# A third PSUM bank from another pool, and a new layout and order for the second FFN product of a decoder layer

## The chip, the cores and the metric

The kernel runs on one NeuronCore of a Trainium2 chip. Its engines run side by side, each with an instruction queue of its own that it works through in order: TensorE (PE in the profile, its weight loads PEld) multiplies matrices into PSUM, VectorE (DVE) and ScalarE (ACT) work element by element on PSUM and SBUF, GpSimd (POOL) on SBUF alone, and SyncE (SP) issues DMA transfers, which ScalarE and GpSimd can issue too. The metric is the device time of one execution in microseconds, as the median of several runs.

## The reference

The reference computes one decoder layer on a sequence of 1024 positions and 1024 channels in float32: RMS norm, an input projection, two kinds of attention with gates, an output projection with a residual, and then the feed-forward part, which is what this document is about:

```python
h2 = rms_norm(x, norm_ffn_g[layer])
gu = h2 @ w_ffn_in[layer]                       # (1024, 1024) @ (1024, 5632)
x = x + (jax.nn.silu(gu[..., :D_FF]) * gu[..., D_FF:]) @ w_ffn_down[layer]
return rms_norm(x, norm_final_g)                # D_FF = 2816
```

So the first FFN product makes a gate g and a value u for each of 2816 hidden channels, the hidden activation is a = silu(g) * u, and the second FFN product takes a, (1024, 2816), back to 1024 channels.

## The kernel before

**Precision.** Each float32 operand is split into a high part, which ScalarE rounds to the format that TensorE takes (L99), and a low part, the rest, which VectorE subtracts (L100). A product is three matmuls: high x high, high x low, low x high. A matmul here takes 128 x 128 weights and 512 columns and fills one PSUM bank. There are eight banks: six in the pool `psd` (tag d, the function `pd()`), two in `psf` (tag f). The pair `psf` is used for transposes and, earlier in the kernel, for the projections of the gates.

**First FFN product.** The hidden channels are worked in 22 blocks of 128 (j = 0 to 21). Blocks 0 and 1 are computed plainly. Each block from 2 on, the function `up`, uses a scheme with seven half-size products instead of eight, on the split activations (`hT_t`), and on sums of them (`tT`: T2, T3, T4) and of the weights (S12, S34, made by GpSimd and split). The seven products, each 12 matmuls (L299), accumulate in three banks b1, b2, b3; between them VectorE and ScalarE read the banks:

- b1: A1 x B11, copied to c1 (L1122); then A1 x B21 is added, and from b1 come a sigmoid (L1130) and a multiplication by it (tile sg, L1037), the last reader of b1;
- b2: S12 x T2, then v2 = b2 + c1; S34 x T3, then v3 = b2 + c1; A22 x T4, then a1 = b2 + c1;
- b3: S12 x T1, then a2 = b3 + v3; S34 x B22, then b3 + v2, the second half's gate.

The results go to DRAM: for blocks 2 to 17 in pairs to `left_dram`, as seven kinds of operands that are sums of quarters (`left_rows`, tile f1, L1162), for blocks 0, 1 and 18 to 21 to `a_dram`. The planner that lays out the instructions overlaps neighbouring blocks: on TensorE the first product of block j+2 comes between the products of block j and those of block j+1.

**Second FFN product.** First the plain rows of block 0: eight row tiles by two halves, 16 banks of three matmuls (L103 to L105), each copied out of its bank into the accumulator `acc` by ScalarE (first half, L1222) or VectorE (second half, L1224). Then seven products (function `product`, L1257), each over eight pairs of blocks: for each pair the left half and the right half of a raw operand are loaded by SyncE (L1246, L1252), split, and multiplied into four banks, 12 matmuls. After each product `into` adds its four banks to one or two quarters of `acc` on VectorE (L1227). During the second of them the residual is added (L1236). Last come the plain rows of blocks 1 and 18 to 21, with the final norm.

**Memory and order.** Pools are stacks, on the left or on the right of SBUF. A pool opened where others have been closed lies over their tiles, and `reuse_waits="tile"` makes each of its tiles wait for those old tiles that it overlaps, and for no other. Before the pool `down` there lay, from the left: `hT_t` (64 KB of each partition), `tT` (48 KB), and the pool `up` (s, s34, a22, c1, v2, v3, sg1, two buffers of a, and the S12 operands, 52 KB together); on the right f1 (8 KB) and two raw weights of odd blocks (8 KB). In the kernel before, `down` starts with `acc` as one tile of 32 KB, over `hT_t`; raw operands (seven buffers of 4 KB) and split ones (11 of 2 x 4 KB) follow as they come. The order on each engine is made by a planner, from the order in the program, what depends on what, and its own estimate of times. `tc.issue_after(ins)` tells it that an instruction may not come before `ins` on its engine's queue.

Of the kernel before, what the change touches and what calls it, by code (L numbers as in the profile page):

```python
# [8 lines left out]
F32 = mybir.dt.float32  # L9
F32R = mybir.dt.float32r  # L10
I32 = mybir.dt.int32
AF = mybir.ActivationFunctionType
ALU = mybir.AluOpType
PSUM = bass.MemoryType.PSUM

P = 128
D = 1024
S = 1024
KT = D // P
NT = S // P  # L20
HALF = 512
# [26 lines left out]
def layer_kernel(  # L48
# [16 lines left out]
    nc = tc.nc  # L65
# [3 lines left out]
    def pool_of(name, bufs, side="left"):  # L69
        return tc.tile_pool(name=name, bufs=bufs, side=side, reuse_waits="tile")  # L70
# [20 lines left out]
    def nm(s):  # L91
        uid[0] += 1
        return f"{s}_{uid[0]}"

    def pd():
        return psd.tile([P, HALF], F32, tag="d", name=nm("pd"))
# [169 lines left out]
    def reserve(pool, *places):  # L266
        for tag, shape, dtype, bufs in places:
            for _ in range(bufs):
                pool.tile([P] + shape, dtype, tag=tag, name=nm(tag), bufs=bufs)
# [836 lines left out]
    with pool_of("up", 1) as fpool:  # L1106
        reserve(fpool, ("s", [KT, P], F32, 2), *[("s34" + n, [KT, P], F32R, 1) for n in "hl"],
                *[("a22" + n, [4, P], F32R, 1) for n in "hl"],
                *[(n, [HALF], F32, 1) for n in ("c1", "v2", "v3", "sg1")], ("a", [S], F32, 2))

        def tmp(n):
            return fpool.tile([P, HALF], F32, tag=n, name=nm(n), bufs=1)

        def up(j, todo, half):
            A1, S12, S34, A22 = left_side(fpool, *(odd if j == PLAIN + 1 else raws(j)), 2, 1)
            b1, b2, b3 = pd(), pd(), pd()
            a = fpool.tile([P, S], F32, tag="a", name=nm("a"), bufs=2)
            a1, a2 = a[:, :HALF], a[:, HALF:]
            c1, v2, v3, sg1 = [tmp(n) for n in ("c1", "v2", "v3", "sg1")]
            prod(b1, A1[:, :4], B11, True)  # L1120
            with tc.issue_after(s12_hi[0].ins) if j == PLAIN else ExitStack():
                nc.scalar.activation(out=c1[:], in_=b1[:], func=AF.Copy)  # L1122
            prod(b2, S12[:, 4:], T2, True)
            vi = from_bank(v2[:], b2, c1)
            if todo:
                with tc.issue_after(vi.ins):
                    left_rows(*todo, 1)
            prod(b1, A1[:, 4:], B21)

            nc.scalar.activation(out=sg1[:], in_=b1[:], func=AF.Sigmoid)  # L1130
            gi = from_bank(sg1[:], b1, sg1, ALU.mult)
            if todo:
                with tc.issue_after(gi.ins):
                    left_rows(*todo, 2)
            prod(b2, S34[:, :4], T3)
            from_bank(v3[:], b2, c1)
            prod(b3, S12[:, :4], T1, True)
            ai = from_bank(a2, b3, v3)
            if half:
                with tc.issue_after(ai.ins):  # L1140
                    left_rows(None, half, None, 0)
            prod(b2, A22, T4)
            from_bank(a1, b2, c1)
            nc.gpsimd.tensor_tensor(out=a1, in0=a1, in1=sg1[:], op=ALU.mult)
            prod(b3, S34[:, 4:], B22)
            gt2, sg2 = tmp("v3"), tmp("sg1")
            from_bank(gt2[:], b3, v2)
            nc.scalar.activation(out=sg2[:], in_=gt2[:], func=AF.Sigmoid)
            nc.gpsimd.tensor_tensor(out=sg2[:], in0=gt2[:], in1=sg2[:], op=ALU.mult)
            nc.gpsimd.tensor_tensor(out=a2, in0=a2, in1=sg2[:], op=ALU.mult)  # L1150
            return a[:].rearrange("p (b c) -> p b c", b=2)

        def left_rows(n, p, q, part):

            if part == 0:
                ops = [(2, p[:, 0], p[:, 1], ALU.subtract)]
            elif part == 1:
                ops = [(0, p[:, 1], q[:, 1], ALU.add)]
            else:
                ops = [(1, f1[:, 0], p[:, 0], ALU.subtract), (3, q[:, 0], f1[:, 1], ALU.subtract)]  # L1160
            for i, x_, y_, op in ops:
                nc.vector.tensor_tensor(out=f1[:, i], in0=x_, in1=y_, op=op)  # L1162
            if part == 2:
                nc.gpsimd.dma_start(out=rows_of(left_dram[n, 3:7]), in_=f1[:])

        todo, one = None, None
        for j in range(PLAIN, NFF):
            n, second = divmod(j - 2, 2)
            a = up(j, todo, one if second and n < len(TWO_ROWS) else None)
            todo = None  # L1170
            if n >= len(TWO_ROWS):
                nc.gpsimd.dma_start(out=a_dram[j], in_=a.rearrange("p b c -> p (b c)"))
            elif second:
                nc.gpsimd.dma_start(out=rows_of(left_dram[n, 1:3]), in_=a)
                todo = (n, one, a)
            else:
                nc.gpsimd.dma_start(out=left_dram[n, 0], in_=a[:, 0])
                one = a
# [3 lines left out]
    h_ctx.__exit__(None, None, None)  # L1182


    with pool_of("down", 1) as fpool:
        acc = fpool.tile([P, NT, D], F32, name="acc", bufs=1)

        def operand(raw):

            w = Pair(*[fpool.tile([P, 2, HALF], F32R, tag="o" + n, name=nm("o" + n), bufs=11) for n in "hl"])  # L1190
            split(w.hi[:], w.lo[:], raw)
            return w

        def raw_rows():
            return fpool.tile([P, 2, HALF], F32, tag="or", name=nm("raw"), bufs=7)

        def whole(j):

# [11 lines left out]
        def plain_rows(js, evac):  # L1210
            both = [whole(j) for j in js]
            for t in range(NT):
                for ch in range(2):
                    pt = pd()
                    for n, (a, w) in enumerate(both):
                        mm3(pt[:], a[:, t * P:(t + 1) * P], w[:, ch * HALF:(ch + 1) * HALF],
                            n == 0, n == len(both) - 1)
                    evac(t, ch, acc[:, t, ch * HALF:(ch + 1) * HALF], pt)

        def first_rows(t, ch, out, pt):  # L1220
            if ch == 0:
                nc.scalar.activation(out=out, in_=pt[:], func=AF.Copy)  # L1222
            else:
                nc.vector.tensor_copy(out, pt[:])  # L1224

        def add(out, bank, op=ALU.add):
            nc.vector.tensor_tensor(out=out, in0=out, in1=bank[:], op=op)  # L1227

        plain_rows([0], first_rows)

# [2 lines left out]
        def residual(t):  # L1233
            xr = fpool.tile([P, D], F32, tag="xf", name=nm("xr"), bufs=3)
            last_xr[0] = nc.gpsimd.dma_start(out=xr[:], in_=x1_dram[t])
            nc.vector.tensor_tensor(out=acc[:, t], in0=acc[:, t], in1=xr[:], op=ALU.add)  # L1236

        def product(left, right, banks, each=None):


            new = banks is None
            banks = banks or [pd() for _ in range(NT // 2)]
            last = len(TWO_ROWS) - 1
            for n, two in enumerate(TWO_ROWS):
                raw = raw_rows()
                nc.sync.dma_start(out=raw[:, 0], in_=left_dram[n, left])  # L1246
                if isinstance(right, tuple):
                    j, b = two[right[0]], right[1]
                    src = w_ffn_down[j * P:(j + 1) * P, b * HALF:(b + 1) * HALF]
                else:  # L1250
                    src = right_dram[n, right]
                nc.sync.dma_start(out=raw[:, 1], in_=src)  # L1252
                w = operand(raw[:])
                for t, bank in enumerate(banks):
                    l, r = w[:, 0, t * P:(t + 1) * P], w[:, 1]
                    for i, (p, q) in enumerate(((l.hi, r.hi), (l.hi, r.lo), (l.lo, r.hi))):
                        nc.tensor.matmul(bank[:], p, q, start=new and n == 0 and i == 0, stop=n == last and i == 2,  # L1257
                                         skip_group_check=True)
                if each:
                    each(n)  # L1260
            return banks

        def into(banks, *blocks, op=ALU.add):
            for t, bank in enumerate(banks):
                for th, ch in blocks:
                    add(acc[:, th * NT // 2 + t, ch * HALF:(ch + 1) * HALF], bank, op)

        A11, A12, A22, S1, S2, S3, S4 = range(7)
        T1, T3, T4, T2 = range(4)
# [17 lines left out]
        def last_rows(t, ch, out, pt):  # L1287
# [7 lines left out]
                return  # L1295
            ss = small.tile([P, 1], F32, tag="ss", name=nm("ss"))
            nc.vector.tensor_tensor(out=ss[:], in0=parts[0][:], in1=parts[1][:], op=ALU.add)
            nc.vector.tensor_tensor(out=xf[:], in0=acc[:, t, :], in1=gainf[:], op=ALU.mult)
            r = rstd(ss, True)
            for c in range(2):  # L1300
                cs = slice(c * HALF, (c + 1) * HALF)
# [40 lines left out]
```

## Time and profile before

| | |
|---|---|
| median of 3 runs | 1468.48 us (1467.93 to 1469.89) |
| profiled execution, its own time | 1468.82 us |
| span in its profile | 1467.1 us |
| TensorE busy | 1441.3 us, 98% of the span |
| VectorE, ScalarE, GpSimd busy | 956.6, 553.3, 504.1 us |
| blocks of the first product with seven products | about 854 to 1241 us |
| seven products of the second | about 1250 to 1404 us |

A row of the profile names a line of the kernel (L299), an engine, an operation and tiles, written `out<-in`. In the rows in order of time the first number is the start in us from the beginning of the span, the second the duration, and what stands in brackets is how long the engine had been idle before it and what ended that. In the chain of waits a row is a start, a duration and an instruction, followed by `x` and a count where several in a row are merged. Tiles of one tag show one name, so v2 and v3 are both `v`.

### The profile page before, as it was taken

To read this page: it belongs to the slowest core of one execution; us is meant where nothing else is said; L and a number is where in the kernel's file an instruction comes from. 1 tells how busy PE (TensorE), PEld (TensorE's weight loads), DVE (VectorE), ACT (ScalarE), POOL (GpSimd) and SP (SyncE) were. 2 spreads that over 40 slices of the span, in tenths; PEclk is the share of its full clock that TensorE was granted. 3 is DMA by queue.
4 is the path that set the end of the run, shared out by engine and by line. 5 is a ranking of instruction groups with operands and counts; after the bars stand their busy time and mean duration, and the time that the engine had idled before them with its cause. 6 is when DMAs were issued, how large, how long until landed. Compare 5 with 4: busy or idle time off the path is not lost. (4 is left out here: it accounts for less than half of the span.)

```text
span 1467.1 us, 18389 instructions
## 1 busy us (share of the span) xinstructions
PE 1441.3 (98%) x6876; PEld 1162.5 (79%) x6876; DVE 956.6 (65%) x1336; ACT 553.3 (38%) x824; POOL 504.1 (34%) x438
## 2 busy tenths in 40 slices
PE   8999999999999999999999999999999999999997
PEld 7898888877677776788887778888888887788886
DVE  6484654359889999846528865555556555876555
ACT  5333332236656423354315432223223323543333
POOL 1020444535533321110146166666666665000000
PEclk9999999999999999999999999999999999999999
DMA  7232454575543461265759312323233332986502
GB/s 231 72 101 79 144 166 124 139 212 130 129 122 102 168 206 36 80 233 170 293 201 367 106 58 80 107 93 104 98 108 108 107 103 88 384 287 210 164 29 86
DMA packets 165785, 213.58 MB, mean 146 GB/s; under 512 B 13760, under 2 KB 115136, under 8 KB 165440
## 3 DMA queue, kind: packets, MB, share of 16 engines
q1 hardware_dynamic: 129376, 119.06, 26.2%
q0 software_dynamic: 15344, 55.59, 10.4%
q10 hardware_dynamic: 20976, 37.76, 8.2%
q8 instruction: 54, 0.88, 0.3%
q14 instruction: 35, 0.29, 0.1%
HBM read 146.32 MB, written 66.06 MB: 145 GB/s over the span
## 5 line engine op out<-in xcount | busy, mean ns | idle before, releaser
L299 PE MATMUL pd<-hT_t,wh 128*128 128x512 f32 x856 | 265.0, 390 | 1.4 <-DVE sg L1037 0.6
L299 PE MATMUL pd<-tT,wh 128*128 128x512 f32 x768 | 235.1, 389 | 0.7 <-ACT wh L99 0.6
L100 DVE TENSOR_TENSOR wl<-wr,wh 128x1024 fp32r<-128x1024 f32 (+2 forms) x110 | 131.2, 1194 | 127.9 <-ACT wh L99 127.3
L99 ACT ACTIVATE wh<-wr 128x1024 fp32r<-128x1024 f32 (+2 forms) x110 | 95.4, 867 | 285.6 <-PE pd L299 166.2
L299 PEld LDWEIGHTS pd<-hT_t,wh 128*128 128x128 f32 x856 | 160.0, 188 | 37.8 <-DVE sg L1037 4.7
L299 PEld LDWEIGHTS pd<-tT,wh 128*128 128x128 f32 x768 | 144.0, 188 | 31.4 <-ACT wh L99 1.0
L299 PE MATMUL pd<-hT_t,wl 128*128 128x512 f32 x428 | 166.5, 389 | 0.0
L299 PE MATMUL pd<-tT,wl 128*128 128x512 f32 x384 | 147.6, 389 | 0.0
L105 PE MATMUL pf<-hT_t,wl 128*128 128x512 f32 x288 | 114.5, 398 | 0.0
L103 PE MATMUL pf<-hT_t,wh 128*128 128x512 f32 x288 | 114.1, 396 | 0.0
L104 PE MATMUL pf<-hT_t,wh 128*128 128x512 f32 x288 | 113.7, 395 | 0.0
L100 DVE TENSOR_TENSOR ol<-raw,oh 128x1024 fp32r<-128x1024 f32 x66 | 79.6, 1223 | 45.8 <-ACT oh L99 38.5
L99 ACT ACTIVATE wh<-s 128x1024 fp32r<-128x1024 f32 x58 | 61.4, 1060 | 118.3 <-POOL s L286 91.3
L285 POOL TENSOR_TENSOR s<-wr 128x512 f32<-128x512 f32 x29 | 60.4, 2084 | 123.9 <-DMA wr<-in_w_in_dram 71.0
L99 ACT ACTIVATE oh<-raw 128x1024 fp32r<-128x1024 f32 x66 | 69.2, 1060 | 87.4 <-PE pd L1257 66.8
L299 PEld LDWEIGHTS pd<-hT_t,wl 128*128 128x128 f32 x428 | 80.3, 188 | 16.9
L100 DVE TENSOR_TENSOR wl<-s,wh 128x1024 fp32r<-128x1024 f32 x58 | 72.2, 1246 | 32.3 <-ACT wh L99 32.3
L1257 PE MATMUL pd<-ol,oh 128*128 128x512 f32 x224 | 87.2, 390 | 1.7 <-DVE ol L100 1.7
L1257 PE MATMUL pd<-oh,ol 128*128 128x512 f32 x224 | 86.3, 389 | 0.0
L984 POOL TENSOR_TENSOR r<-r 128x512 f32<-128x512 f32 x32 | 44.2, 1391 | 120.7 <-DMA r<-in_w_ffn_down_dram 119.3
L299 PEld LDWEIGHTS pd<-tT,wl 128*128 128x128 f32 x384 | 72.1, 188 | 15.0
L1257 PE MATMUL pd<-oh 128*128 128x512 f32 x224 | 83.9, 389 | 0.0
(277 smaller groups left out, 3068.4 us busy)
## 6 DMA issues: line engine op xcount, KB each, us to landing
wr<-in_w_in_dram SPq DMA_DIRECT2D x46, 512.0 KB, 4.7
wr<-in_w_ffn_in_dram SPq DMA_DIRECT2D x44, 512.0 KB, 3.8
raw<-left_dram SPq DMA_DIRECT2D x56, 256.0 KB, 5.3
g_dram<-fst ACTq DMA_DIRECT2D x32, 256.0 KB, 2.5
land<-g_dram SPq DMA_DIRECT2D x16, 512.0 KB, 3.4
r<-in_w_ffn_down_dram SPq DMA_DIRECT2D x8, 1024.0 KB, 10.4
right_dram<-r POOLq DMA_DIRECT2D x8, 1024.0 KB, 6.2
left_dram<-f POOLq DMA_DIRECT2D x8, 1024.0 KB, 4.7
```

The costliest lines, as they stand in the source:

```text
L99: last_hi[0] = nc.scalar.activation(out=hi, in_=src, func=AF.Copy)
L100: return nc.vector.tensor_tensor(out=lo, in0=src, in1=hi.bitcast(F32), op=ALU.subtract)
L103: nc.tensor.matmul(psum, w.hi, m.hi, start=start, stop=False)
L104: nc.tensor.matmul(psum, w.hi, m.lo, start=False, stop=False)
L105: last_mm[0] = nc.tensor.matmul(psum, w.lo, m.hi, start=False, stop=stop)
L285: nc.gpsimd.tensor_tensor(out=s12[:, :4], in0=u1, in1=u2, op=ALU.add)
L299: last_mm[0] = nc.tensor.matmul(bank[:], p, q, start=first and k == 0 and n == 0, stop=k == 3 and n == 2, skip_group_check=True)
L984: nc.gpsimd.tensor_tensor(out=out, in0=p, in1=q, op=ALU.subtract)
L1257: nc.tensor.matmul(bank[:], p, q, start=new and n == 0 and i == 0, stop=n == last and i == 2, skip_group_check=True)
```

## The change

The third bank b3 of each block with seven products is taken from `psf`. In the second FFN product the accumulator becomes eight tiles of one row tile each: rows 0 and 1 lie in a new pool `early` on the right, beside two raw buffers; in the left pool the places are reserved in a fixed sequence: rows 2 to 5, twelve split operands high and twelve low, two raw buffers, the tiles for the residual and the gain, rows 6 and 7, and five raw buffers, of which one is skipped on the first turn. Raw buffers are nine instead of seven, split operands twelve instead of eleven. And the splits get a told order: in the first product the split of operand n (0 to 7) comes, on each of the two engines, after that engine's copy of the plain rows' row tile 2n + 1 (at most the last, 7); in the later products the low halves from the fourth operand on come after the last add of the product before.

```diff
         def up(j, todo, half):
-            b1, b2, b3 = pd(), pd(), pd()
+            b1, b2, b3 = pd(), pd(), psf.tile([P, HALF], F32, tag="f", name=nm("pf"))
...
-    with pool_of("down", 1) as fpool:
-        acc = fpool.tile([P, NT, D], F32, name="acc", bufs=1)
+    with pool_of("down", 1) as fpool, pool_of("early", 1, side="right") as epool:
+        def rows(pool, *ts):
+            for t in ts:
+                acc[t] = pool.tile([P, D], F32, tag=f"acc{t}", name=nm("acc"), bufs=1)
+
+        acc = [None] * NT
+        rows(epool, 0, 1)
+        rows(fpool, 2, 3, 4, 5)
+        reserve(fpool, *[("o" + n, [2, HALF], F32R, 12) for n in "hl"], ("os", [2, HALF], F32, 2),
+                ("xf", [D], F32, 3), ("gain", [D], F32, 1))
+        rows(fpool, 6, 7)
+        reserve(fpool, ("or", [2, HALF], F32, 5))
+        fpool.tile([P, 2, HALF], F32, tag="or", name=nm("raw"), bufs=5)
...
-            w = Pair(*[fpool.tile([P, 2, HALF], F32R, tag="o" + n, name=nm("o" + n), bufs=11) for n in "hl"])
+            w = Pair(*[fpool.tile([P, 2, HALF], F32R, tag="o" + n, name=nm("o" + n), bufs=12) for n in "hl"])
...
+        turn = [0]
+
         def raw_rows():
-            return fpool.tile([P, 2, HALF], F32, tag="or", name=nm("raw"), bufs=7)
+            places = [(epool, "oe", 2)] * 2 + [(fpool, "os", 2)] * 2 + [(fpool, "or", 5)] * 5
+            pool, tag, bufs = places[turn[0] % 9]
+            turn[0] += 1
+            return pool.tile([P, 2, HALF], F32, tag=tag, name=nm("raw"), bufs=bufs)
...
+        emptied = [[], []]
+
         def first_rows(t, ch, out, pt):
             if ch == 0:
-                nc.scalar.activation(out=out, in_=pt[:], func=AF.Copy)
+                emptied[0].append(nc.scalar.activation(out=out, in_=pt[:], func=AF.Copy))
             else:
-                nc.vector.tensor_copy(out, pt[:])
+                emptied[1].append(nc.vector.tensor_copy(out, pt[:]))
...
         def product(left, right, banks, each=None):
...
-                w = operand(raw[:])
+                after = [q[min(2 * n + 1, NT - 1)].ins for q in emptied]
+                if n >= 3 and last_add[0]:
+                    after[1] = last_add[0].ins
+                with tc.issue_after(after[0]), tc.issue_after(after[1]):
+                    w = operand(raw[:])
...
         def into(banks, *blocks, op=ALU.add):
             for t, bank in enumerate(banks):
                 for th, ch in blocks:
-                    add(acc[:, th * NT // 2 + t, ch * HALF:(ch + 1) * HALF], bank, op)
+                    last_add[0] = add(acc[th * NT // 2 + t][:, ch * HALF:(ch + 1) * HALF], bank, op)
```

The other lines of the diff only write `acc[t][...]` for `acc[:, t, ...]`.

More of the change, by code (lines that the diff above doesn't have):

```diff
@@ L1217, in plain_rows @@
                             n == 0, n == len(both) - 1)
-                    evac(t, ch, acc[:, t, ch * HALF:(ch + 1) * HALF], pt)
+                    evac(t, ch, acc[t][:, ch * HALF:(ch + 1) * HALF], pt)
+        emptied = [[], []]
         def first_rows(t, ch, out, pt):
             if ch == 0:
-                nc.scalar.activation(out=out, in_=pt[:], func=AF.Copy)
+                emptied[0].append(nc.scalar.activation(out=out, in_=pt[:], func=AF.Copy))
             else:
-                nc.vector.tensor_copy(out, pt[:])
+                emptied[1].append(nc.vector.tensor_copy(out, pt[:]))
+        last_add = [None]
         def add(out, bank, op=ALU.add):
-            nc.vector.tensor_tensor(out=out, in0=out, in1=bank[:], op=op)
+            return nc.vector.tensor_tensor(out=out, in0=out, in1=bank[:], op=op)
         plain_rows([0], first_rows)
@@ L1235, in residual @@
             last_xr[0] = nc.gpsimd.dma_start(out=xr[:], in_=x1_dram[t])
-            nc.vector.tensor_tensor(out=acc[:, t], in0=acc[:, t], in1=xr[:], op=ALU.add)
+            nc.vector.tensor_tensor(out=acc[t][:], in0=acc[t][:], in1=xr[:], op=ALU.add)
         def product(left, right, banks, each=None):
@@ L1297, in last_rows @@
             nc.vector.tensor_tensor(out=ss[:], in0=parts[0][:], in1=parts[1][:], op=ALU.add)
-            nc.vector.tensor_tensor(out=xf[:], in0=acc[:, t, :], in1=gainf[:], op=ALU.mult)
+            nc.vector.tensor_tensor(out=xf[:], in0=acc[t][:], in1=gainf[:], op=ALU.mult)
             r = rstd(ss, True)
```

## The prediction

> **What bounds the kernel now.** I read the page first, then TensorE's instructions in order of time, looking for places where two matmuls start further apart than usual, then what VectorE, ScalarE, GpSimd and the DMA queues did at those places. The page's head and the start of its chain:
>
> ```profile
> span 1467.1 us, 18389 instructions
> PE 1441.3 (98%) x6876; PEld 1162.5 (79%) x6876; DVE 956.6 (65%) x1336; ACT 553.3 (38%) x824; POOL 504.1 (34%) x438
> ```
>
> TensorE is busy for 98%, so only its gaps can be won. A busy share hides short gaps, because one matmul of 0.39 us overlaps the next. The pitch is what counts. The chain of waits has one long run of the second FFN product that nothing interrupts, and the steady part of the first product beside it:
>
> ```profile
> 952.01 32.72 PE pd L299 x143
> ...
> 989.83 0.61 DVE sg L1037
> 990.49 32.74 PE pd L299 x143
> ...
> 1182.99 49.27 PE pd L299 x216
> ...
> 1254.25 149.92 PE pd L1257 x660
> ```
>
> 660 matmuls start within 149.92 us less one duration (0.39) plus one pitch: 0.227 us each. Two blocks j of the first product are 2 x 7 x 12 = 168 matmuls, 38.12 us at that pitch, but the chain comes back to the same VectorE instruction after 990.49 - 952.01 = 38.48. So 0.36 us is lost every two blocks, at one place, seven times from 952.01 to 1182.99. TensorE's instructions in order of time show it, and a larger case one pair earlier:
>
> ```profile
> 951.51 0.39 PE L299 MATMUL pd<-hT_t,wl 128*128 128x512 f32 x1
> 952.01 0.73 PE L299 MATMUL pd<-hT_t,wh 128*128 128x512 f32 x2
> 952.58 0.39 PE L299 MATMUL pd<-hT_t,wl 128*128 128x512 f32 x1
> ...
> 912.54 0.39 PE L299 MATMUL pd<-hT_t,wl 128*128 128x512 f32 x1
> 913.52 0.73 PE L299 MATMUL pd<-hT_t,wh 128*128 128x512 f32 x2 [0.59 <-DVE sg L1037]
> ```
>
> 951.51 to 952.01 is 0.50 instead of 0.23, and the two matmuls after it take 0.57 to the next instead of 0.45: 0.39 together, which agrees with the period's 0.36. At 912.54 it is 0.75 + 0.11 = 0.86.
>
> **The wait in the first product.** VectorE at that place:
>
> ```profile
> 947.37 2.29 DVE L100 TENSOR_TENSOR wl<-wr,wh 128x1024 fp32r<-128x1024 f32 x1 [3.69 <-ACT wh L99]
> 949.58 1.77 DVE L1162 TENSOR_TENSOR f<-a,a 128x512 f32<-128x512 f32 x1
> 951.28 0.68 DVE L1037 TENSOR_TENSOR sg<-pd,sg 128x512 f32<-128x512 f32 x1
> 951.88 1.51 DVE L1162 TENSOR_TENSOR f<-f,a 128x512 f32<-128x512 f32 x1
> 953.31 0.68 DVE L1037 TENSOR_TENSOR v<-pd,c 128x512 f32<-128x512 f32 x1
> ...
> 955.11 1.21 DVE L100 TENSOR_TENSOR wl<-s,wh 128x1024 fp32r<-128x1024 f32 x1
> ```
>
> The multiplication that ends at 951.96 is the last reader of a block's bank b1, and in every other block it stands behind a wl and an f of the left rows. With six banks in turn and three per block, the b1 of block j+2 is the b1 of block j, so its first product waits for exactly this reader; 0.05 us after it ends the matmul starts.
>
> *Part 1, b3 from the gates' pair.* No instruction is added or removed. b1 and b2 now go round six banks alone, so a bank comes back after three blocks, and the reader that freed it is one block (19 us) older. b3 goes round two banks and comes back after two blocks, as before; nothing else draws on that pair here. What is next: the product after this one, the last into b2, needs the v that ends at 953.99. Without the wait the first product starts at 951.74, twelve matmuls later it is 954.46, so 0.47 is left. The weights it reads (wl, done at 949.66) are ready. Gain: 7 x 0.37 + 0.86 = 3.45 us. Bounds: if the next wait took all, 0; and the planner may now start something earlier still, for which I add nothing.
>
> **The start of the second product.** TensorE's instructions:
>
> ```profile
> 1233.91 0.39 PE L105 MATMUL pd<-wh,wl 128*128 128x512 f32 x1
> 1234.28 0.50 PE L103 MATMUL pd<-wh,wh 128*128 128x512 f32 x1
> ...
> 1241.01 0.39 PE L105 MATMUL pd<-wh,wl 128*128 128x512 f32 x1
> 1241.50 0.50 PE L103 MATMUL pd<-wh,wh 128*128 128x512 f32 x1
> ...
> 1242.06 0.40 PE L105 MATMUL pd<-wh,wl 128*128 128x512 f32 x1
> 1242.71 0.50 PE L103 MATMUL pd<-wh,wh 128*128 128x512 f32 x1 [0.24 <-ACT acc L1222]
> ...
> 1252.12 0.39 PE L1257 MATMUL pd<-oh 128*128 128x512 f32 x1
> 1254.25 0.50 PE L1257 MATMUL pd<-ol,oh 128*128 128x512 f32 x1 [1.74 <-DVE ol L100]
> 1254.59 0.40 PE L1257 MATMUL pd<-oh,ol 128*128 128x512 f32 x1
> ```
>
> Over the pitch of 0.227, with 0.11 for the slow matmul after each (1254.25 to 1254.59 is 0.34): 0.25 at 1233.91, 0.37 at 1241.01, 0.53 at 1242.06 and 2.01 at 1252.12: 3.16 us. What they wait for, on VectorE, ScalarE, GpSimd and SyncE:
>
> ```profile
> 1252.97 1.23 DVE L100 TENSOR_TENSOR ol<-raw,oh 128x1024 fp32r<-128x1024 f32 x1 [5.17 <-DMA raw<-left_dram]
> ...
> 1246.43 1.37 DVE L1224 COPY acc<-pd 128x512 f32<-128x512 f32 x2
> ...
> 1241.54 0.63 ACT L1148 ACTIVATE sg<-v 128x512 f32<-128x512 f32 x1 [8.04 <-DVE v L1037]
> 1242.08 2.23 ACT L1222 ACTIVATE acc<-pd 128x512 f32<-128x512 f32 x4
> 1244.20 1.05 ACT L99 ACTIVATE oh<-raw 128x1024 fp32r<-128x1024 f32 x1
> ...
> 1245.20 0.60 POOL L1172 DMA_DIRECT2D a_dram<-a  x1 [0.30 <-POOL a L1150]
> ...
> 1240.74 0.33 SPq L1246 DMA_DIRECT2D raw<-left_dram  x1
> ...
> DMA to landing us min/median/max: 2.7/3.3/7.6
> ```
>
> The last row is that of the tensor a_dram. Its slowest transfer, 7.6 us, is the store issued at 1245.20, which lands at 1252.8, and VectorE's second split starts at 1252.97. The row names a raw load, but that load had landed long before: the split's low half lies where that last `a` lay, and cannot be written until the store has read it. The store is slow because the raw loads, released all together at 1240.74 by the last read of hT, run beside it.
>
> *Part 2, the layout.* Rows 0 and 1 of the accumulator and two raw buffers lie on the right, over f1 and the odd blocks' raw weights. By the code these are done with once the last block's weights are split, before the plain rows of 1233.91, while hT is read until 1240.73; so their four banks can be emptied while the first product still runs, and no longer behind the four copies at 1242.08. Two raw buffers lie over `s` and four over the S12 operands, done with by then too. So the operands of the whole first product, eight (2 x 256 KB each), can be loaded before 1240.74, where the DMA engines are nearly idle, and the store at 1245.20 no longer competes:
>
> ```profile
> 1217.00:1232.00 15.00, 15.00 (x68) 12.43 (x67) 9.20 (x10) 4.48 (x6) 6.88 (x5) 1.00 0.09 35
> ...
> 1250.00:1258.00 8.00, 6.26 (x28) 4.84 (x27) 5.03 (x6) 2.74 (x5) 0.00 (x0) 1.00 1.04 413
> ...
> 1272.00:1295.00 23.00, 23.00 (x104) 19.02 (x103) 23.00 (x23) 11.46 (x11) 3.18 (x6) 1.00 1.04 391
> ```
>
> (This view has a stretch, its length, then busy time of TensorE, its weight loads, VectorE, ScalarE and GpSimd; the last three columns are TensorE's granted clock, full in each, DMA share and GB/s.) At 413 GB/s the 4 MB take 10 us, and the 15 us before 1232 move only 35 GB/s. SyncE's queue has nothing behind these loads that TensorE needs sooner. The space of the last `a` now belongs to the raw buffer that is used ninth, so it holds up a load for the next product, wanted 20 us later. The split operands lie over hT and tT and can't be written before 1240.73; the first is wanted by TensorE at about 1248.5 (its twelfth matmul is now at 1252.12, the first eleven pitches before, 1249.6, and 1.15 us of waits before it go). All four waits go: 3.16 us. Lower bound 0, if another wait ends there.
>
> *Part 3, the told order.* Between 1240.7 and 1248.5 ScalarE has a sigmoid (0.63), six copies (0.56 each by the row above), and three splits (1.05): 7.2 of 7.8 us. VectorE has one sum (0.69, as the copies), six copies (0.69 each) and three splits of 1.23: 8.5, and the third split isn't wanted before 1253.9. TensorE has four emptied banks in hand, 12 matmuls or 2.7 us, so neither holds it up. I cost the order at nothing; without that cover it would cost 0.7 us.
>
> *A rule of the Trainium skill.* VectorE's wl took 2.29 us at 947.37 and 1.21 at 955.11 for the same shape. The Trainium skill (SBUF — State Buffer, Who interferes with whom) says that a VectorE instruction with two SBUF inputs contends with a GpSimd instruction that reads SBUF, and the trace's two durations agree. By that rule the first split, moved beside GpSimd's last products before 1245.20, would take 1.06 us longer, and with the cover above the sum would lose some 0.3 us of its 6.6.
>
> **The sum.** 3.45 + 3.16 = 6.6 us. The profiled execution took 1468.82 us (span 1467.1 and 1.7 around it), 0.34 over the median of 1468.48 and inside the runs' 1467.93 to 1469.89. 1468.82 - 6.6 = 1462.2, my forecast; from the median it would be 1461.9.
>
> **Rivals.** *Only one half comes true:* about 1465.3. For it: the planner lays the instructions out anew, and a copy or a split that it puts behind a waiting one gives a wait back. Against it: both halves have cover worked out above.
>
> *Nothing is won, 1466 to 1471:* every wait is replaced by the next. In the first product that needs VectorE's v to come 0.47 us + 0.37 later; one more f (1.51 to 1.77) ahead of it would do. In the second, ScalarE's 7.2 of 7.8 us leaves little.
>
> *Slower, the told order starves TensorE at each change of product.* From the fourth operand on, VectorE may split only after the last add of the product before. At the worst change now:
>
> ```profile
> 1316.94 1.28 DVE L1227 TENSOR_TENSOR acc<-acc,pd 128x512 f32<-128x512 f32 x2 [0.85 <-PE pd L1257]
> ...
> 1319.28 3.67 DVE L1227 TENSOR_TENSOR acc<-acc,pd 128x512 f32<-128x512 f32 x6
> ```
>
> The adds end at 1322.95. The fourth operand is wanted 36 matmuls (8.2 us) and one more pitch after the product's start at about 1317 (the first add is released as the product before ends), 1325.4; a split of 1.22 after the adds is ready at 1324.2. That is 1.2 us of margin where I expect most need, and more where there are four adds instead of eight. It decides once the adds end 7 us or more after the start. To end 2.9 us slower than before it must cost 6.6 + 2.9 = 9.5 us, 1.6 at each of six changes: 1471.7. VectorE is full from 1272 to 1295 (the third of the rows by stretch; the residual adds), which speaks for it at one change, not at six.
>
> **How the numbers follow.** A kernel like this can be told from no change from about 0.2%, 2.9 us, on. Forecast 0.62 (own range 1461 to 1464); one half 0.16, split evenly by the bound at 1465.5; nothing won 0.12; slower 0.10. So faster 0.70, same 0.20, slower 0.10. The range reaches from 1460.5 (a wait I haven't counted goes too, and the runs' spread) to 1467.0, which takes in the half case and part of the third.
>
> **What would show it.** Right: two blocks repeat every 38.1 us; no TensorE start waits for sg L1037; first raw loads issued before 1235; splits one to three done when the plain rows end; the run of the second product without a gap over 0.3 us. Wrong: a new gap before the tT product behind v L1037; ol L100 late at a product's fourth operand; a changed order of the products in a block.

## The result and the profile after

The changed kernel took 1462.41 us (median of 6 runs, 1460.11 to 1465.28), beside 1468.53 us (6 runs, 1466.38 to 1469.89) for the kernel before on the same chip. The ratio is 0.9952, with a 95% interval of 0.9940 to 0.9965: 7.0 us less, between 5.1 and 8.8. The forecast was 1462.2.

The head of the page of the changed kernel; its profiled execution took 1464.02 us:

```profile
span 1462.3 us, 18377 instructions
PE 1439.0 (98%) x6876; PEld 1165.4 (80%) x6876; DVE 956.4 (65%) x1336; ACT 554.3 (38%) x824; POOL 505.1 (35%) x438
```

The same matmuls run, and the busy share reads 98% as before. The two spans differ by only 4.8 us, less than the gain. Where each execution enters the part that the change touches tells why. TensorE's instructions in order of time, of the kernel before:

```profile
851.61 0.61 PE L299 MATMUL pd<-hT_t,wh 128*128 128x512 f32 x2
...
1249.62 0.39 PE L1257 MATMUL pd<-oh 128*128 128x512 f32 x1
...
1403.78 0.39 PE L1257 MATMUL pd<-oh,ol 128*128 128x512 f32 x1
```

The same three landmarks after the change, with the rows in which the forecast looked for its first step between them:

```profile
853.88 0.61 PE L299 MATMUL pd<-hT_t,wh 128*128 128x512 f32 x2
...
953.12 0.62 PE L299 MATMUL pd<-hT_t,wh 128*128 128x512 f32 x2
...
955.84 0.62 PE L299 MATMUL pd<-tT,wh 128*128 128x512 f32 x2
...
1246.88 0.39 PE L1281 MATMUL pd<-oh 128*128 128x512 f32 x1
...
1398.97 0.39 PE L1281 MATMUL pd<-oh,ol 128*128 128x512 f32 x1
```

The changed kernel's execution came 2.3 us later to the first of them, in code that is the same in both (the last section shows where). From there to the first matmul of the second product it needs 1246.88 - 853.88 = 393.00 us instead of 398.01, and from that to the last matmul of the seven products 152.09 instead of 154.16. So 5.0 + 2.1 = 7.1 us are gone, which is what the interval has. Below these two lengths are called **stretch one** and **stretch two**; each kernel's are worked out in the same way from the start times of the same matmuls.

The chain of waits of the changed kernel:

```profile
949.65 2.27 PE pd L299 x10
...
987.73 2.27 PE pd L299 x10
```

VectorE's `sg` no longer stands in it, and two blocks repeat every 38.08 us. VectorE and ScalarE in order of time, at that place and at the start of the second product:

```profile
952.65 0.68 DVE L1037 TENSOR_TENSOR sg<-pd,sg 128x512 f32<-128x512 f32 x1
953.25 1.51 DVE L1162 TENSOR_TENSOR f<-f,a 128x512 f32<-128x512 f32 x1
954.69 0.68 DVE L1037 TENSOR_TENSOR v<-pd,c 128x512 f32<-128x512 f32 x1
...
1232.12 0.60 ACT L1240 ACTIVATE acc<-pd 128x512 f32<-128x512 f32 x1 [0.16 <-PE pd L105]
...
1243.90 2.36 DVE L100 TENSOR_TENSOR ol<-raw,oh 128x1024 fp32r<-128x1024 f32 x2 [0.21 <-ACT oh L99]
```

The block's first product now starts at 953.12, while the `sg` that it used to wait for runs until 953.33. At the start of the second product the first copies run from 1232 on, while hT is still read, and two operands are split by 1246.26, before the first matmul wants them. (The forecast had the third done by the end of the plain rows too; its low half is ready at 1247.99, 1.1 us after that end, and holds nothing up.)

SyncE's queue after the change, and GpSimd's store:

```profile
1228.34 0.43 SPq L1272 DMA_DIRECT2D raw<-in_w_ffn_down_dram  x1
1247.26 0.33 SPq L1266 DMA_DIRECT2D raw<-left_dram  x1
...
1244.05 0.60 POOL L1172 DMA_DIRECT2D a_dram<-a  x1 [0.30 <-POOL a L1150]
```

Here the trace differs from the forecast. Four operands are loaded early, not eight. The fifth operand's load stands behind the store of the last `a`, issued at 1244.05 and landed at 1247.07, and goes out at 1247.26.

### The profile page after: what moved, and what is told of

The parts are those of the page before. It is cut to its first block, busy times and chain, and to the rows that moved or that the text cites. A ratio compares the mean times of both kernels' runs of the same rounds, so it can differ in the third digit from the quotient of the medians.

```text
span 1462.3 us, 18377 instructions
## 1 busy us (share of the span) xinstructions
PE 1439.0 (98%) x6876; PEld 1165.4 (80%) x6876; DVE 956.4 (65%) x1336; ACT 554.3 (38%) x824; POOL 505.1 (35%) x438
## 4 chain that ended last, share of the span: by engine, by line
PE 87%; DVE 7%; issue 2%; POOL 2%; ACT 1%; DMA 1%; SPq 0%; ACTq 0%; DVEq 0%; POOLq 0%
PE pd L299 30%; PE pd L1281 10%; PE pf L299 7%; PE pd L103 7%; PE pd L104 6%; PE pd L105 6%; PE pf L104 3%; PE pf L105 3%; PE pf L103 3%; PE pd L711 1%; PE pd L197 1%; PE pd L200 1%; PE pd L196 1%; PE pd L660 1%; PE pd L661 1%
## 5 line engine op out<-in xcount | busy, mean ns | idle before, releaser
L299 PE MATMUL pd<-hT_t,wh 128*128 128x512 f32 x536 | 165.4, 389 | 0.0
L299 PEld LDWEIGHTS pd<-hT_t,wh 128*128 128x128 f32 x536 | 100.5, 188 | 21.1 <-ACT cc L325 0.2
L103 PE MATMUL pf<-hT_t,wh 128*128 128x512 f32 x288 | 113.8, 395 | 0.0
L104 PE MATMUL pf<-hT_t,wh 128*128 128x512 f32 x288 | 113.5, 394 | 0.0
L299 PE MATMUL pd<-hT_t,wl 128*128 128x512 f32 x268 | 104.3, 389 | 0.0
L299 PE MATMUL pf<-hT_t,wh 128*128 128x512 f32 x320 | 98.7, 389 | 0.0
L100 DVE TENSOR_TENSOR ol<-raw,oh 128x1024 fp32r<-128x1024 f32 x66 | 76.5, 1220 | 6.4 <-ACT oh L99 5.8
```

Source lines behind the costliest of these rows:

```text
L100: return nc.vector.tensor_tensor(out=lo, in0=src, in1=hi.bitcast(F32), op=ALU.subtract)
L103: nc.tensor.matmul(psum, w.hi, m.hi, start=start, stop=False)
L104: nc.tensor.matmul(psum, w.hi, m.lo, start=False, stop=False)
L299: last_mm[0] = nc.tensor.matmul(bank[:], p, q, start=first and k == 0 and n == 0, stop=k == 3 and n == 2, skip_group_check=True)
```

## The experiments

| kernel | time, us | ratio to before, 95% interval | stretch one | stretch two |
|---|---|---|---|---|
| before | 1468.53 | | 398.01 | 154.16 |
| changed | 1462.41 | 0.9952 (0.9940 to 0.9965) | 393.00 | 152.09 |
| b3 from the pair alone | 1468.63 | 0.9993 (0.9982 to 1.0004) | 394.62 | 158.21 |
| layout and order, b3 as before | 1464.53 | 0.9963 (0.9949 to 0.9976) | 396.98 | 152.09 |
| order alone | 1470.45 | 0.9998 (0.9987 to 1.0009) | 397.99 | 157.14 |
| b1 instead of b3 from the pair | 1476.60 | 1.0039 (1.0026 to 1.0052) | 407.96 | 152.09 |
| changed, without the order | 1467.61 | 0.9984 (0.9971 to 0.9998) | 393.00 | 156.58 |
| changed, order of the first product only | 1466.85 | 0.9979 (0.9969 to 0.9990) | 393.04 | 156.77 |
| changed, order of the later products only | 1461.61 | 0.9943 (0.9929 to 0.9957) | 393.03 | 152.09 |
| changed, last `a`'s place used ninth | 1461.97 | 0.9952 (0.9936 to 0.9967) | 393.03 | 152.09 |
| changed, last `a`'s place used first | 1473.00 | 1.0028 (1.0019 to 1.0038) | 401.24 | 155.27 |

Each ratio is to runs of the kernel before on the same chip, whose median moved by up to 1.4 us from chip to chip; the medians of the table are to be read with that. The row of the order of the first product only leaves out one of twelve executions, which took 5988 us. The stretches are those of one execution each.

**Part 1 alone.** The kernel before, with one line of the change.

```diff
-            b1, b2, b3 = pd(), pd(), pd()
+            b1, b2, b3 = pd(), pd(), psf.tile([P, HALF], F32, tag="f", name=nm("pf"))
```

> The kernel before with part 1 alone: b3 of each block comes from the gates' pair, the second product is as it was. Theory (bank reuse): the wait for the reader of b1 goes in all of the steady blocks and in the first of them (7 x 0.37 + 0.86 = 3.45 us), the four waits at the start of the second product stay (about 3.2 us), so about 1465.1 us and a period of 38.1 us for two blocks. Rival (the next wait takes its place): the period stays at 38.5 us and the time at 1468.5.

The period fell to 38.1 us, and stretch one by 3.4. But stretch two became 4.1 us longer, and the time is the same as before. TensorE in order of time, at the start of the second product:

```profile
1236.65 0.39 PE L105 MATMUL pd<-wh,wl 128*128 128x512 f32 x1
1238.35 0.50 PE L103 MATMUL pd<-wh,wh 128*128 128x512 f32 x1 [1.31 <-ACT acc L1222]
...
1245.98 0.39 PE L1257 MATMUL pd<-oh 128*128 128x512 f32 x1
1250.43 0.50 PE L1257 MATMUL pd<-ol,oh 128*128 128x512 f32 x1 [4.06 <-DVE ol L100]
```

GpSimd's store, the row of the tensor a_dram, and VectorE:

```profile
1240.84 0.59 POOL L1172 DMA_DIRECT2D a_dram<-a  x1 [0.30 <-POOL a L1150]
...
DMA to landing us min/median/max: 2.6/3.3/8.1
...
1249.15 1.23 DVE L100 TENSOR_TENSOR ol<-raw,oh 128x1024 fp32r<-128x1024 f32 x1 [6.34 <-issue]
1250.29 1.28 DVE L1224 COPY acc<-pd 128x512 f32<-128x512 f32 x2
```

Two waits grew. Among the plain rows the wait for ScalarE's copies is 1.70 us from start to start; it was 0.65 (1242.06 to 1242.71). And the old stall at the start of the second product is 4.45 us instead of 2.13. The store itself moved up with the rest, from 1245.20 to 1240.84; it takes 8.1 us and lands at 1249.0, and VectorE's second split starts 0.2 us later. But one more copy of the plain rows now stands behind that split on VectorE, three instead of two, so its bank comes free late as well, and TensorE gets through 4 matmuls of the first of the seven products before it stands still, where it got through 12 before. After the gap it is slow for 3 us (the last section). So part 1's gain is real but was taken back at the next waits: the two halves of the change aren't worth their sum one by one.

**The layout and the order, without part 1.** The changed kernel with that line put back.

> The changed kernel with part 1 undone: b3 from the six banks again, layout and told order of the second product as changed. Theory: the period of two blocks is 38.5 us again, the gaps of TensorE at the start of the second product are gone, so about 1465.4 us. Rival (the second product's gain needs the freed banks): gaps of 1 us or more come back between the plain rows, because their banks are still held by the last block; 1466.5 or more.

Its chain of waits:

```profile
949.08 0.61 DVE sg L1037
949.74 32.73 PE pd L299 x143
...
988.23 32.72 PE pd L299 x143
```

And TensorE at the plain rows:

```profile
1231.91 0.50 PE L103 MATMUL pd<-wh,wh 128*128 128x512 f32 x1
```

The old wait is back with a period of 38.5 us. Of the four waits at the start of the second product three are gone. The first stays: the matmul at 1231.91 starts 0.36 us after the one ahead of it, right behind the last block's `sg`, which ends at 1231.86. With part 1 alone this wait is gone, so it belongs to part 1: it too is a wait for the last reader of b1. The two stretches are 1.0 + 2.1 = 3.1 us shorter than before, as expected. The ratio says 5.4 us with an interval of 3.5 to 7.5. The profiled execution was 5.4 us shorter than that of the kernel before, and 2.3 us of this lie ahead of the first landmark (849.35 instead of 851.61), in code that is the same; why the other executions were as fast stays open.

**The order alone.** The two conditions on the kernel before, with its one accumulator and seven raw buffers.

> The kernel before with the told order of the splits alone (old layout, b3 from the six banks). Theory: the second split still waits for the store of the last a, so the gap of about 2 us at the start of the second product stays and the time is 1468 to 1468.5 us. Rival (the order brings the second product's gain): the gap goes, 1466.5 or less. Second rival (the order starves TensorE at each change of product): gaps at the fourth operand, over 1469.5.

TensorE in order of time:

```profile
1249.74 0.39 PE L1265 MATMUL pd<-oh 128*128 128x512 f32 x1
1252.12 0.50 PE L1265 MATMUL pd<-ol,oh 128*128 128x512 f32 x1 [2.00 <-DVE ol L100]
```

The wait for the second low half stays, 2.38 us from start to start. In this execution slow matmuls follow it and another gap of 1.2 us at 1294, which make stretch two 3.0 us longer than before; the ratio's interval (1.9 us less to 1.3 more) doesn't show that for the other executions. The time is the same as before: the order wins nothing where the buffers don't let the splits run early.

**The other bank from the pair.** The changed kernel with b1 in place of b3.

```diff
-            b1, b2, b3 = pd(), pd(), psf.tile([P, HALF], F32, tag="f", name=nm("pf"))
+            b1, b2, b3 = psf.tile([P, HALF], F32, tag="f", name=nm("pf")), pd(), pd()
```

> The changed kernel, but b1 instead of b3 is taken from the gates' pair, so b1 again comes back after two blocks and b2 and b3 after three. As many banks are in use. Theory (it is the reuse distance of b1 that counts): the wait for the reader of b1 is back, 38.5 us for two blocks, 1465.9 us. Rival (any relief of the six banks does it): 38.1 us for two blocks, 1462.4 us.

The direction was as the theory said, the size was not: the period is 40.06 us. TensorE, VectorE and ScalarE in order of time:

```profile
952.23 0.39 PE L299 MATMUL pd<-hT_t,wl 128*128 128x512 f32 x1
954.30 0.74 PE L299 MATMUL pf<-hT_t,wh 128*128 128x512 f32 x2 [1.69 <-DVE sg L1037]
...
992.29 0.39 PE L299 MATMUL pd<-hT_t,wl 128*128 128x512 f32 x1
...
947.44 1.06 ACT L99 ACTIVATE wh<-wr 128x1024 fp32r<-128x1024 f32 x1 [4.25 <-PE pf L299]
...
949.32 1.76 DVE L1162 TENSOR_TENSOR f<-a,a 128x512 f32<-128x512 f32 x1 [4.93 <-POOL a L1150]
951.01 2.64 DVE L100 TENSOR_TENSOR wl<-wr,wh 128x1024 fp32r<-128x1024 f32 x1
953.57 0.68 DVE L1037 TENSOR_TENSOR sg<-pf,sg 128x512 f32<-128x512 f32 x1
```

The `sg` wait is back, because b1 again comes round after two blocks. It is 2.07 us instead of 0.50 from start to start, because the planner put `f` (L1162) ahead of the weight split `wl` in every other block. `wl` could have started when ScalarE's `wh` was done, at 948.50; instead VectorE stood at `f` until GpSimd's `a` came at 949.3, and `wl` moved back by 2.5 us; `sg`, which stands behind both either way, comes 1.6 us later against TensorE. Nothing in the change asks for that exchange of two neighbours. That it is what makes the wait longer is read from this queue; no run puts the two back. The two stretches together are 7.9 us longer than before, a little more than the 3.8 to 7.6 us of the ratio.

**The changed kernel without the told order.**

```diff
-                with tc.issue_after(after[0]), tc.issue_after(after[1]):
-                    w = operand(raw[:])
+                w = operand(raw[:])
```

> The changed kernel without the told order of the splits; banks and layout as changed. Theory: the order was costed at nothing, so 1462.4 us and no new gap on TensorE. Rival (without it the planner puts splits ahead of the copies out of the banks): gaps between the plain rows at the start of the second product, 0.5 to 2 us, 1463 to 1464.5.

This expectation was wrong: stretch two is 4.5 us longer than in the changed kernel. TensorE and then VectorE in order of time, at the change from the first to the second of the seven products:

```profile
1268.31 0.39 PE L1277 MATMUL pd<-oh,ol 128*128 128x512 f32 x1
1271.32 0.76 PE L1277 MATMUL pd<-oh 128*128 128x512 f32 x1 [2.61 <-DVE acc L1247]
...
1265.21 3.96 DVE L100 TENSOR_TENSOR ol<-raw,oh 128x1024 fp32r<-128x1024 f32 x3 [0.85 <-ACT oh L99]
1269.35 1.23 DVE L100 TENSOR_TENSOR ol<-raw,oh 128x1024 fp32r<-128x1024 f32 x1 [0.17 <-ACT oh L99]
1270.49 0.68 DVE L1247 TENSOR_TENSOR acc<-acc,pd 128x512 f32<-128x512 f32 x1
```

The first matmul of the second of the seven needs the bank that the first of them filled, and VectorE must add that bank to the accumulator first. Without the order VectorE does four more low halves of the next product between 1265.21 and 1270.58, and only then the add. In the changed kernel the add starts at 1266.80, as soon as the bank is full (row below).

**Which half of the order.** Two kernels, each with one of the two conditions. The first keeps only the order of the splits among the copies of the plain rows:

```diff
-                if n >= 3 and last_add[0]:
-                    after[1] = last_add[0].ins
```

> The changed kernel with the told order kept in the first of the seven products, but no rule that low halves from the fourth operand on come after the last add. Theory: 1462.4 us, as the changed kernel, since each product's fourth operand has 3.8 us and more in hand there; the adds end later after a change of product (6 us instead of 3.5 at the change from the third to the fourth). Rival (late adds hold up banks): gaps at changes of product, 1463 or more.

> The changed kernel without the first half of the told order: the splits of the first product are no longer told to come after the copies of the plain rows; the low halves (and now the high ones too, after ScalarE's last copy) from the fourth operand on still come after the last add of the product before. Theory: the order is worth its 4.5 us only at the change from the first product to the second, where the adds would otherwise stand behind ten splits; the copies of the plain rows go first anyway, because their banks are ready before the raw operands can be split (the first split can't write before 1242, the copies are ready from 1232 on). Then this kernel takes the same as the changed one, 1462.4 (ratio to before 0.9952), with no wait of TensorE between 1240 and 1270. Rival: without it the planner puts splits ahead of the last copies, the four banks of the first product come free late, and a wait of 1 to 2 us for the tile acc appears between 1240 and 1248, as the kernel with part 1 alone had 1.70 us there: 1463.4 to 1464.4, and up to 1466 if TensorE slows down after it.

The first, against its expectation, again waits 3.2 us from start to start for the add, and its stretch two is 156.77. The second has the changed kernel's stretches to within 0.03 us. So the order among the copies does nothing that can be measured, and the 4.5 us hang on one condition: from the fourth operand on, the split comes after the last add of the product before.

**The place of the last `a`.** As SyncE's queue shows, the raw buffer that has to wait for the last `a` was the fifth in use, not the ninth as forecast. One kernel moves it to the ninth use, by putting row 7 of the accumulator behind the five buffers; another makes it the first.

```diff
# ninth
-        rows(fpool, 6, 7)
+        rows(fpool, 6)
         reserve(fpool, ("or", [2, HALF], F32, 5))
-        fpool.tile([P, 2, HALF], F32, tag="or", name=nm("raw"), bufs=5)
+        rows(fpool, 7)
# first
-            places = [(epool, "oe", 2)] * 2 + [(fpool, "os", 2)] * 2 + [(fpool, "or", 5)] * 5
+            places = [(fpool, "or", 5)] * 5 + [(epool, "oe", 2)] * 2 + [(fpool, "os", 2)] * 2
```

> The changed kernel with row 7 of the accumulator placed behind the five raw buffers, so that the raw buffer over the last a is the ninth in use and not the fifth. Theory: loads five to eight are issued at about 1235 instead of 1247, the fifth split is ready some 10 us earlier, and the time stays at 1462.4 us because the changed kernel had 1.1 us in hand there. Rival (the late loads cost something elsewhere, by contention with the residual's loads): up to 1 us less.

> The changed kernel with the raw buffers taken in another turn: the first operand's lies over the last a. Theory (the store of the last a gates what lies over it): the first load is issued when the store has landed, at about 1247, lands 3 us later, is split in 1.1 us, so TensorE stands still for 4 to 6 us before the second product: 1467 to 1468.5 us. Rival (the store was not the cause): 1462.4 us.

SyncE's queue with that place used ninth:

```profile
1235.63 0.43 SPq L1272 DMA_DIRECT2D raw<-in_w_ffn_down_dram  x1
1243.63 0.33 SPq L1266 DMA_DIRECT2D raw<-left_dram  x1
```

All eight operands' loads are issued by 1235.63, only the ninth waits until 1243.63, and nothing is won: the changed kernel's fifth operand was in time anyway. With the place used first, TensorE and SyncE:

```profile
1244.79 0.39 PE L105 MATMUL pd<-wh,wl 128*128 128x512 f32 x1
1253.22 1.22 PE L1281 MATMUL pd<-oh 128*128 128x512 f32 x2 [8.04 <-ACT oh L99]
...
1207.69 0.43 SPq L1272 DMA_DIRECT2D raw<-in_w_ffn_down_dram  x1
1245.40 0.33 SPq L1266 DMA_DIRECT2D raw<-left_dram  x1
```

SyncE stands at the first operand's load from 1208 to 1245.40, with the loads behind it, and TensorE waits 8.4 us. It costs 11.4 us in the two stretches, more than was expected. The load landed 6.0 us after its issue, beside those behind it, and not 3, so the gap itself was longer; and slow matmuls follow it, which the expectation left out: 3.2 us in stretch two.

## Why the prediction was right

**Part 1, forecast 3.45 us: right in mechanism and size.** The period was to be 38.12 and is 38.08. What is next was named too: 0.47 us in hand before the product that needs `v`. In the rows after, `v` ends at 955.37 and that product starts at 955.84: 0.47. The forecast is short by one wait: the 0.25 us at 1233.91, which it counted to part 2, is the last of the waits for `sg`; the sum isn't touched by that. In the kernel before, `sg` ends at 1234.22 and the matmul starts at 1234.28; with part 1 alone the wait is gone, and without part 1 it stays. The rival "nothing is won" had named one more `f` ahead of `v`. The kernel with b1 in the pair shows what a place in that queue can do, with an `f` ahead of `wl` and so a later `sg`: 1.6 us per two blocks, where 0.4 was to be won.

**Part 2, forecast 3.16 us: right in size, with two wrong steps.** All four waits went, though the first of them, 0.25 us, by part 1 (above); the layout alone won 3.1 us where 2.9 were left to it. Stretch two lost 2.07 us for the 2.01 forecast. Stretch one lost 5.01 for 3.45 + 0.25 + 0.37 + 0.53 = 4.60; the 0.4 left over is the true pitch (38.08 over 168 matmuls is 0.2267, not 0.227) and the matmuls after each gap that were a few hundredths long. The sum, 6.6, is 7.1 in the trace. The other wrong step is "the space of the last `a` now belongs to the raw buffer that is used ninth": it was the fifth, so half of the first product's loads did wait for the store. It cost nothing. The four operands ahead were loaded by then, so the store landed at 1247.1, 3.0 us after its issue, instead of 7.6. In the kernels above the store takes 7.6 to 8.1 us wherever the loads run beside it (before, part 1 alone, order alone), and 3.0 in all the others. The fifth operand's low half was ready at 1256.64, and TensorE came to that operand at 1257.76. The kernel with eight early loads confirms it.

**Part 3, forecast at nothing: the right sum by the wrong question.** I asked what the order costs, and it costs nothing. I didn't ask what the new layout would do without it: 4.5 us of the gain would be lost at the first change of product. Why it is the new layout that needs the order stays open. In the kernel before, too, VectorE does six low halves of the second of the seven products before the first add, but it is through with them 0.4 us before the bank is full. In the changed kernel without the order it does seven, and the add starts at 1270.49, more than 3 us late.

**The rivals.** *Slower, by the order:* refuted, and in fact the other way round. VectorE in the changed kernel, at the first change and at the one that I took as the worst:

```profile
1266.80 1.37 DVE L1247 TENSOR_TENSOR acc<-acc,pd 128x512 f32<-128x512 f32 x2 [2.10 <-PE pd L1281]
...
1310.77 4.87 DVE L1247 TENSOR_TENSOR acc<-acc,pd 128x512 f32<-128x512 f32 x8 [8.21 <-PE pd L1281]
1315.56 6.90 DVE L100 TENSOR_TENSOR ol<-raw,oh 128x1024 fp32r<-128x1024 f32 x6
```

VectorE idles before both groups of adds and starts them at once; the first low half after them, the fourth operand's, is done 1.22 us after 1315.56, at 1316.78, and by count of matmuls TensorE comes to that operand at 1320.32. That is 3.5 us in hand for the 1.2 forecast, which rested on adds that VectorE did in two lots; without splits in between they end earlier. *One half, 1465.3:* as a result it was refuted, but its reason, a copy behind a waiting split, is part of what spoils part 1 alone. I had priced the halves as if each kept its own gain. Alone, part 1 makes the two stretches 0.7 us longer (in time, it lies between 2.6 us less and 0.6 more), the layout with its order makes them 3.1 shorter, both together 7.1.

**The rule of the Trainium skill** on VectorE beside GpSimd wasn't put to the test: the first two splits, 2.36 us together, begin at 1243.90, after GpSimd's last product (which ends at 1243.75, before its store), and ran at their usual length. The 0.3 us that the forecast gave as its price don't follow from the numbers beside it: VectorE's 8.5 + 1.06 us are 1.8 us more than the 7.8, inside the 2.7 us that TensorE had in hand.

## What to carry to other kernels

A wait that is taken away moves what follows and may change the planner's order at the next wait, so remove consecutive stalls together, and don't call a half useless because it wins nothing alone: part 1 alone gave back all that it had won. When more buffers let an engine work ahead, say which of its instructions others wait for, and order the rest behind those: here one such condition carried 4.5 of 7 us. Before buffers are laid over old tiles, work out which use in turn gets the place that comes free last; first cost 11 us, fifth and ninth cost nothing.

## What the hardware did that I had not expected

After some gaps TensorE runs at half its clock for about 3 us. The view by stretches (a stretch, its length, busy time of TensorE, its weight loads, VectorE, ScalarE and GpSimd, then TensorE's granted clock, DMA share and GB/s), first of the kernel before, after its gap of 2.13 us from start to start:

```profile
1254.25:1258.00 3.75, 3.75 (x16) 3.11 (x17) 3.75 (x5) 0.90 (x2) 0.00 (x0) 1.00 1.03 410
```

The order alone, after a gap of 2.38 us that ended at 1252.12:

```profile
1252.10:1253.60 1.50, 1.48 (x6) 1.24 (x7) 1.50 (x3) 1.06 (x1) 0.00 (x0) 1.00 1.02 410
1253.60:1257.00 3.40, 3.40 (x9) 2.63 (x8) 3.07 (x3) 0.97 (x1) 0.00 (x0) 0.51 1.04 400
```

The changed kernel without the order, after its gap of 3.01 us:

```profile
1271.32:1274.70 3.38, 3.38 (x8) 2.70 (x9) 3.38 (x5) 2.73 (x3) 0.37 (x1) 0.50 1.06 388
```

After 2.13 us the clock stayed full, 16 matmuls in 3.75 us. After 2.38 us it was halved 1.5 us later for 3.4 us, and after 3.01 us at once: 8 matmuls in 3.38 us, 0.43 each, some 1.6 us lost beside the gap itself. The gap of 4.45 us of part 1 alone was followed by the same (0.50 for 3.0 us), that of 8.43 us by 6 us of it, and that of 3.19 us of the order of the first product only by 3.4 us of it, 1.2 us later. The Trainium skill (TensorE: Matmul & The Clock Gate, Part 1: The HAM clock gate) has the clock halved after an idle window of some 3.4 us that runs free of the kernel, until a busy one. The half clock and its length agree with these rows; that a gap of 2.38 us can be enough, with TensorE idle for 2.00 us of it, is shorter than the page's figure. Gaps near 2 us go both ways. The kernel with b1 from the pair has seven of 2.07 us, and the clock is full after each; the first:

```profile
954.30:958.00 3.70, 3.70 (x16) 3.09 (x17) 3.48 (x5) 0.00 (x0) 0.77 (x1) 1.00 0.09 33
```

But in the same execution a gap of 2.10 us that ends at 798.47, ahead of the first landmark and among short transposes, was followed by a clock of 0.50 from 799.8 to 803.0. At the same place the changed kernel's execution had a gap of 2.71 us and 0.51 for 3.2 us after it, where that of the kernel before had a gap of 1.09 us and the full clock: that is where its 2.3 us come from. What made the gap longer there stays open. So in these executions a gap of about 2 us mostly cost its own length, and each of the five from 2.38 us on that follow the first landmark cost more, the one of 3.01 us 1.6 us more.
